# A two-layer streaming encoder on one core: the second layer's mixer is recorded and laid out as one planned order

## The chip, the core and the metric

The kernel runs on one core of one Trainium2 chip. The metric is device time of one execution in microseconds (us). All numbers are float32; matrix products run on TensorE (PE) in the fp32r form, and each product of float32 quality is made of three such products of split operands (high by high, high by low, low by high). VectorE is called DVE, ScalarE ACT, GpSimd POOL and SyncE SP, as in the profile. SP issues the weight loads; POOL issues small transfers.

## The reference, cut to what matters

One sequence of 512 tokens and 1024 features goes through two layers. Each layer adds a mixer, a cross-attention to 256 memory rows, and a gated ConvFFN to the stream `x`; only the mixers differ.

```
# layer 0: eight forgetting heads, four differential heads, one output projection
p = p1 - lam * p2
d_out = rms_norm(d_out, subln) * (1.0 - lambda_init)
mixed = concat(fox_out, d_out) @ w_out
# layer 1: mLSTM, four heads, chunkwise
qk = silu(causal_depthwise_conv(qk_pre, conv_qk))
h = mlstm_chunkwise(q, k, v, i_pre, log_f)
h = merge_heads(rms_norm(h, head_norm)) * sigmoid(og)
mixed = h @ w_out
```

So in both mixers a head's output is scaled by a root of its own mean square: four times in layer 0 (the differential heads), four times in layer 1.

## The kernel before, in words

**Stages.** `run` executes, per layer, a mixer (`mix0` or `mix1`) and then `rest` (cross-attention and ConvFFN). In the profiled execution `mix0` lies at about 0 to 253 us, `rest` of layer 0 at 253 to 714, `mix1` at 714 to 932 and `rest` of layer 1 at 932 to 1405.

**Tiles.** Activations stand as eight tiles of 128 features by 512 tokens, each as a high and a low part (`xh`, `xl`). A weight block of 128 by 1024 is loaded by SP into `raw`, cast by ACT to its high part `wh`, and DVE subtracts for the low part `wl` (`weight`, line 371; three buffers of each). A projection (`p_proj`, line 402) is 24 matmuls of 128x512 into one of four PSUM banks `acc` and is then evacuated by ACT and DVE. `p_proj_tok` (line 430) makes the values, 96 matmuls into all four banks.

**What sets the order.** Two things do. In `rest`, every instruction is a task of a list scheduler (`Sched`, line 180) with costs and due times, and the tasks are issued with `planned(True, 4)`: each instruction of DVE, ACT, POOL and SP then carries an ordering edge to the one before it on its engine, so the program's order is the order written down. In the two mixers a coarser planner (`Plan`, line 86) orders items of PE work with rough costs of the other engines, and issues a whole item at once; where the instructions of an item end up on their engine is then decided by the framework's own scheduler, which may move an instruction ahead of others that it does not depend on.

**The far norm.** `p_far_norm` (line 486) gets a head's 512 scale factors to all partitions by way of DRAM: PE sums squares, DVE makes `z`, POOL the root `y`; POOL issues a small DMA `roots<-y` to DRAM and a second DMA `hrb<-roots` (256 KB) that reads it back to all 128 partitions; then DVE multiplies by `hrb` (in layer 0 the row `ta<-ta,warm,hrb`), ACT casts the high part `mh`, and DVE subtracts for the low part `ml`. There is one buffer `hrb`, so the next copy waits until DVE has read the last. Line 507 calls `follow`: the next instruction on DVE gets an ordering edge to the instruction that was issued last there (or to a named one), so the framework's scheduler cannot move the multiplication ahead of it.

**Softmax of layer 0.** For each head and block of 128 queries PE writes scores to one of two PSUM banks `s`, DVE (the custom row with `sm`, shown as `ISA` in the order of instructions) adds the mask or bias and takes the extreme, ACT exponentiates, DVE takes the reciprocal, PE transposes, ACT or DVE copies to `pt`, and PE weighs the values. `p_qk` makes a head's keys: DVE `tmp<-acc,rb`, four ACT casts `ka`, two DVE subtractions `kb`.

**Mixer of layer 1.** Gate projection (`p_gate`, 16 matmuls), 96 matmuls for the first half of the values, then per head two projections with a convolution on DVE and ACT, two output gates, scores in the transposed form, a denominator and two numerators, a far norm (a near one for the last head), and at the end the output projection. Two blocks of the cross-attention's keys (`p_fill`) stand before the output projection. `p_memory` loads and splits the memory rows for that.

Of the kernel before, what the change touches and what calls it, by code (L numbers as in the profile page):

```python
# [9 lines left out]
F32 = mybir.dt.float32  # L10
# [22 lines left out]
MEM_AT, MEM_STEP = (140.0, 100), (24.0, 16.0)  # L33
FILLS, FILL_AT, FILL_PRIO = 2, (210.0, 140.0), 99
# [41 lines left out]
class Item:  # L76
    def __init__(self, fn, dur, deps, prio, take, free, chain, pre, after, order, load, st):
# [8 lines left out]
class Plan:  # L86
# [11 lines left out]
    def add(self, fn, dur=0.0, deps=(), prio=None, take=(), free=(), chain=(), pre=(), after=0.0, order=(), load=(), st=None, soon=False):  # L98
        it = Item(fn, dur, [d for d in deps if d is not None], len(self.items) if prio is None else prio, take, free, chain, pre, after, order, load, st)
        it.n, it.soon = len(self.items), soon  # L100
        self.items.append(it)
        return it

    def run(self):
        todo = sorted(self.items, key=lambda i: (i.prio, i.n))
        eng, t = self.eng, self.t
        while todo:
# [27 lines left out]
            for e, d in pick.pre:  # L135
                eng[e] = max(eng[e], t - 4.0) + d
            t += pick.dur
# [29 lines left out]
class Task:  # L167
    def __init__(self, eng, dur, fn, deps, prio, take, free, lat, after):
# [3 lines left out]
        self.take, self.free = take, free  # L172
# [3 lines left out]
WAIT = {"DVE": 0.4, "ACT": 0.3}  # L176
ONE, TWO, FORM, THEN = 4, 12, 10.0, (2, 1, 1)
OUT = (0, 4, 1, 5, 2, 6, 3, 7)

class Sched:  # L180
# [3 lines left out]
    def __init__(self, wait={}, **res):  # L184
        self.tasks, self.wait, self.held, self.ahead = [], wait, [], AHEAD
# [16 lines left out]
    def dues(self):  # L202
# [6 lines left out]
        for r, s in self.slots.items():  # L209
            takes = [(t, st) for t in self.tasks for q, st in t.take if q == r]  # L210
            if r == "acc":
                takes = [(None, st) for st in self.held] + takes
# [23 lines left out]
    def run(self):  # L236
# [7 lines left out]
        for t in self.tasks:  # L244
            for r, _ in t.take:
# [4 lines left out]
        while any(todo.values()):  # L250
            best = None
            for e, ts in todo.items():
                able = []
                for t in ts[:120]:
# [9 lines left out]
                    for j, (r, _) in enumerate(t.take):  # L264
                        if want[r][0] is not t:
# [18 lines left out]
            for r, st in t.take:  # L284
                want[r].pop(0)
# [10 lines left out]

class InOrder:
# [3 lines left out]
    def __init__(self, tc, engine):  # L301
        self.tc, self.engine = tc, engine
# [3 lines left out]
    def __getattr__(self, name):  # L306
        issue = getattr(self.engine, name)

        def call(*a, **k):
            i = issue(*a, **k)  # L310
# [7 lines left out]
    def follow(self, after=None):  # L318
        self.next = after or True


class Engines:
    def __init__(self, tc, names):
        self.nc = tc.nc
        self.chains = [InOrder(tc, getattr(tc.nc, n)) for n in names]
# [10 lines left out]

class Builder:
    def __init__(self, tc, t):
        self.tc, self.nc, self.t = tc, Engines(tc, ORDERED), t
# [12 lines left out]
    def til(self, pool, tag, shape=(P, 512), dtype=F32, bufs=None):  # L352
        return pool.tile(list(shape), dtype, tag=tag, name=self.nm(tag), bufs=bufs or 2)

# [47 lines left out]
    def p_proj(self, pl, src, xs, evac, chain, deps=(), kdeps=None, edeps=(), prio=None, n=SEQ, nk=KB8, order=None, etake=(), per=2, eorder=(), load=()):  # L402
# [5 lines left out]
        for c, e in zip(cuts, cuts[1:] + [nk]):  # L408
# [12 lines left out]
            for k in ks:  # L421
# [4 lines left out]
                pre=(("A", 0.12 * nk), ("D", 0.14 * nk)) if first else (), st=st,  # L426
            )
        return pl.add(lambda: evac(st["ps"]), 0, [last, *edeps], prio, take=etake, free=("acc",), chain=chain, order=eorder, load=load, st=st, soon=True)
# [92 lines left out]
    def p_out(self, pl, src, mixed, kdeps, gain, gi, order, prio, reload=False, order0=None):  # L521
# [3 lines left out]
        for m in range(KB8):  # L525
            e = self.p_proj(
                pl, src[m], mixed, lambda ps, m=m: self.xadd(m, ps, reload), (("D", 0.6),), kdeps=kdeps, order=order, prio=prio + m
# [192 lines left out]
    def split_rows(self, pool, *rows):  # L720

        t = pool.tile([P, SEQ], F32R, name=self.nm("rows"))
# [50 lines left out]
    def p_qk(self, pl, dq, dk, par, kdeps, edeps, prio):  # L773

        st = {}
        q = self.p_proj(
            pl, dq, self.xs, lambda ps: st.update(q=self.q_parts(ps)), (("D", 0.66), ("A", 0.52), ("D", 0.6), ("D", 0.6)), load=(("A", 0.52),),
# [3 lines left out]
            pl, dk, self.xs, lambda ps: st.update(k=self.k_parts(ps, par)), (("D", 0.6), ("A", 0.52), ("D", 0.6), ("D", 0.6)), load=(("A", 1.56),),  # L781
# [64 lines left out]

    def p_values(self, pl, src, edeps, prio, kdeps=None, ready=None):
# [28 lines left out]
    def mix0(self):  # L876
        nc, t, tc = self.nc, self.t, self.tc
        with tc.tile_pool(name="mix0", bufs=1, reuse_waits="tile") as mp:
            self.mp = mp
            self.kbt = [[mp.tile([P, 512], F32R, name=f"kb{s}{i}") for i in range(2)] for s in range(2)]  # L880
# [4 lines left out]
            sub8 = self.warm[:, 2:3]  # L885
            dmask = mp.tile([P, 512], F32, name="dmask")
            nc.vector.memset(dmask[:], 0.0)
            nc.vector.memset(dmask[0:64, 448:512], BIG)
            mh, ml = ([None if k in (2, 3) else mp.tile([P, SEQ], F32R, name=f"{n}{k}") for k in range(8)] for n in ("mh", "ml"))
# [4 lines left out]
            self.x = [self.xp.tile([P, SEQ], F32, name=f"x{k}", tag=f"x{k}") for k in range(KB8)]  # L894
# [74 lines left out]
            for h in range(4):  # L969
                p = 10 + 10 * h  # L970
                if h == 0:
                    v, ve = self.p_values(pl, t["dv"], [norm], p - 1, xk, [lambda: vw[1:], second])
                st, qk = self.p_qk(pl, t["dq"][h], t["dk"][h], h % 2, xk, [norm], p)
                pt = {}
                got = pl.add(lambda pt=pt: pt.update(t=self.til(mp, "pt", (P, 1536), bufs=3)), 0, qk, p + SOFT_PRIO, take=("pt",))
                ss, ts = [], []
                for i in range(4):
                    n = P * (i + 1)
                    bias = lambda n=n: dmask[:, 512 - n : 512]
                    r1, a1, b1 = self.p_soft(pl, st, 0, i, bias, qk, p + SOFT_PRIO)  # L980
# [1518 lines left out]
```

## Time and profile before

| | us |
|---|---|
| median of three runs | 1406.52 |
| lowest and highest of them | 1406.43, 1407.12 |
| the profiled execution's own time | 1407.05 |
| span of that execution | 1404.9 |

The span runs from the first instruction to the last; the 2.15 us between it and the execution's own time lie around it. The timeline's rows give start, duration, engine, line, operation, tiles and, in brackets, the idle time of the engine before the row and what ended it. A matmul's shown duration has a modelled end, so two matmuls in flight overlap in the rows; the distance between starts is what tells whether PE was kept waiting. In rows of DMA issues on POOL the shown duration is that of the issue, and the time to landing stands in the DMA view. Helper functions record every instruction under one line (L310), so groups are told apart by tiles.

### The profile page before, as it was taken

How to read it: one execution, taken by the hardware profiler on the slowest of the kernel's cores; microseconds unless marked ns; L12 is line 12 of the kernel's file. 1: busy time of each engine (PE TensorE's matmuls, PEld its weight loads, DVE VectorE, ACT ScalarE, POOL GpSimd, SP SyncE). 2: the span in 40 equal slices, each digit the busy share in tenths (PEclk: the TensorE clock that was granted, in tenths of full speed). 3: DMA queues.
4: the chain of work that ended last, by engine and by line, in shares of the span. 5: the costliest groups of instructions: out<-in, count | busy, mean ns of one | idle time of the engine just before them, and what ended most of it. 6: DMA issues, size and time to landing. Idle time of an engine off the chain costs nothing.

```text
span 1404.9 us, 23512 instructions
## 1 busy us (share of the span) xinstructions
PE 1390.2 (99%) x8876; PEld 1265.2 (90%) x8876; DVE 1186.4 (84%) x2042; ACT 874.4 (62%) x1486; POOL 146.8 (10%) x213
## 2 busy tenths in 40 slices
PE   9999999999999999999999999999999999999998
PEld 8888878899899999999888888989989999999997
DVE  7787786888799999999768876678878999999984
ACT  6797565666576665666456664456656866565555
POOL 0002230010011111011001120001000111110000
PEclk9999999999999999999999999999999999999999
DMA  6225324765567787674333332367464878776522
GB/s 207 91 53 154 117 68 151 246 188 158 158 145 191 211 199 187 151 200 106 86 108 105 129 98 83 120 188 240 136 185 114 196 201 204 182 185 168 154 66 81
DMA packets 80544, 211.06 MB, mean 150 GB/s; under 512 B 8640, under 2 KB 8640, under 8 KB 80432
## 3 DMA queue, kind: packets, MB, share of 16 engines
q1 hardware_dynamic: 63520, 165.02, 36.3%
q0 software_dynamic: 15904, 43.44, 17.7%
q8 instruction: 69, 1.13, 0.3%
q10 hardware_dynamic: 1008, 1.12, 0.2%
q14 instruction: 43, 0.35, 0.1%
HBM read 203.20 MB, written 6.34 MB: 149 GB/s over the span
## 4 chain that ended last, share of the span: by engine, by line
PE 85%; DVE 8%; ACT 3%; issue 2%; DMA 1%; POOL 1%; SPq 0%; POOLq 0%; DVEq 0%; ACTq 0%
PE acc L388 16%; PE acc L390 16%; PE acc L389 16%; PE w L388 4%; PE w L389 4%; PE w L390 4%; PE s L388 3%; PE s L390 3%; PE s L389 3%; PE acc L451 2%; PE acc L452 2%; PE acc L450 2%; DVE wl L310 1%; DVE qc L310 1%; PE w L2275 1%
## 5 line engine op out<-in xcount | busy, mean ns | idle before, releaser
L310 ACT CAST wh<-raw 128x1024 fp32r<-128x1024 f32 (+2 forms) x217 | 222.0, 1026 | 160.9 <-PE acc L389 76.4
L310 DVE TENSOR_TENSOR wl<-raw,wh 128x1024 fp32r<-128x1024 f32 (+2 forms) x217 | 259.6, 1198 | 39.2 <-ACT wh L310 37.9
L388 PE MATMUL acc<-xh,wh 128*128 128x256 f32 (+1 forms) x704 | 228.7, 325 | 0.0
L390 PE MATMUL acc<-xh,wl 128*128 128x256 f32 (+1 forms) x704 | 227.4, 323 | 0.5 <-DVE wl L310 0.5
L389 PE MATMUL acc<-xl,wh 128*128 128x256 f32 (+1 forms) x704 | 227.1, 323 | 0.0
L390 PEld LDWEIGHTS acc<-xh,wl 128*128 128x128 f32 x704 | 134.4, 191 | 9.3 <-DVE wl L310 0.9
L388 PEld LDWEIGHTS acc<-xh,wh 128*128 128x128 f32 x704 | 134.5, 191 | 7.6
L389 PEld LDWEIGHTS acc<-xl,wh 128*128 128x128 f32 x704 | 134.5, 191 | 7.5
L310 DVE SCALAR_TENSOR_TENSOR qc<-va,vec,qc 128x512 f32<-128x512 f32 x176 | 131.8, 749 | 6.9 <-ACT qc L310 4.0
L389 PE MATMUL acc<-f,k 128*128 128x256 f32 x336 | 92.5, 275 | 0.0
L390 PE MATMUL acc<-f,k 128*128 128x256 f32 x336 | 92.5, 275 | 0.0
L388 PE MATMUL acc<-f,k 128*128 128x256 f32 x336 | 92.5, 275 | 0.0
L310 ACT ACTIVATE qc<-va,vec 128x512 f32<-128x512 f32 x88 | 71.1, 812 | 19.2 <-DVE q L310 9.5
L388 PE MATMUL w<-q,wh 128*128 128x512 f32 x208 | 79.1, 380 | 0.6 <-ACT qc L310 0.6
L390 PE MATMUL w<-q,wl 128*128 128x512 f32 x208 | 78.9, 379 | 0.0
L389 PE MATMUL w<-q,wh 128*128 128x512 f32 x208 | 78.9, 379 | 0.0
L310 ACT ACTIVATE u<-acc 128x256 f32<-128x256 f32 x96 | 36.4, 379 | 68.1 <-PE acc L390 66.4
L390 PE MATMUL acc<-mem,wl 128*128 128x256 f32 (+1 forms) x236 | 73.8, 313 | 1.1 <-DVE wl L310 1.1
L388 PE MATMUL acc<-mem,wh 128*128 128x256 f32 (+1 forms) x236 | 73.9, 313 | 0.1
L389 PE MATMUL acc<-mem,wh 128*128 128x256 f32 (+1 forms) x236 | 73.7, 312 | 0.0
L310 DVE TENSOR_TENSOR x<-acc,x 128x512 f32<-128x512 f32 (+1 forms) x43 | 28.0, 653 | 47.2 <-PE acc L390 47.2
L310 ACT CAST k<-xe 128x512 fp32r<-128x512 f32 x84 | 51.0, 614 | 25.4 <-DVE xe L310 10.7
(414 smaller groups left out, 4207.0 us busy)
## 6 DMA issues: line engine op xcount, KB each, us to landing
raw<-in_up_dram SPq DMA_DIRECT2D x46, 512.0 KB, 4.3
raw<-in_down_dram SPq DMA_DIRECT2D x32, 512.0 KB, 4.6
sa<-in_up_dram SPq DMA_DIRECT2D x28, 512.0 KB, 5.1
sa<-in_up_dram POOLq DMA_DIRECT2D x28, 512.0 KB, 6.5
vb<-in_up_dram SPq DMA_DIRECT2D x42, 256.0 KB, 4.0
xe<-in_up_dram POOLq DMA_DIRECT2D x42, 256.0 KB, 4.8
raw<-in_wo_dram SPq DMA_DIRECT2D x16, 512.0 KB, 3.6
raw<-in_xk_dram SPq DMA_DIRECT2D x16, 512.0 KB, 3.9
```

The source lines that it names most:

```text
L310: i = issue(*a, **k)
L388: mm(out, wh, xh, start=first, stop=False, skip_group_check=parts)
L389: mm(out, wh, xl, start=False, stop=False, skip_group_check=parts)
L390: mm(out, wl, xh, start=False, stop=last, skip_group_check=parts)
L450: mm(ps, xh[k][:, ts], wh, start=(k == 0), stop=False)
L451: mm(ps, xh[k][:, ts], wl, start=False, stop=False)
L452: mm(ps, xl[k][:, ts], wh, start=False, stop=(k == 7))
L2275: nc.tensor.matmul(ps[:, lo:], vv[s][:, c], a[:], start=(s == 0), stop=(s == 3))
```

## The change

The text adds a layer between the mixers' code and the engines. `Ref` and `View` stand for tiles that are not yet allocated. A `Recorder` stands in for the four engines and PE: in recording mode it makes a task of every instruction, with costs per engine and kind, dependencies from the tiles' regions, and a ring of buffers per tag; at the end the list scheduler that `rest` uses orders all tasks of all five engines and issues them with `planned(True, 4)`. In direct mode the recorder issues the instruction at once, as before. `BEGIN` sets from which planner time on a mixer is recorded: 1e9 for layer 0, which is never reached, and 0 for layer 1. So `mix0` has a recorder attached but stays in direct mode, and `mix1` is recorded whole.

Beside it: `follow` does nothing while a recorder is attached, in direct mode too; the order numbers of layer 1's items come from tables (`PROJ1`, `SOFT1`, `NORM1`, `GATE1`, `V1`, `EARLIES1`) in place of sums; layer 1's memory rows are loaded at planner time 20 instead of 100, and its two blocks of keys may start at 44 instead of 140; in layer 0 the buffer `kb` is taken from a list instead of by the head's parity. The tables of layer 0 hold the values that the sums gave. No arithmetic changes: each engine has the same instructions in the same numbers, in another order.

```diff
-MEM_AT, MEM_STEP = (140.0, 100), (24.0, 16.0)
-FILLS, FILL_AT, FILL_PRIO = 2, (210.0, 140.0), 99
+MEM_AT, MEM_STEP = (140.0, 20), (24.0, 4.0)
+FILLS, FILL_AT, FILL_PRIO = 2, (210.0, 44.0), 99
...
+SOFT1, NORM1 = [-28, 6.5, 39.5, 58], [11, -7.5, 21.5, 2.5]
...
+BEGIN, EARLY = (1e9, 0.0), 0.0
...
+    def item(self, t, it):
...
+        if self.direct and t >= self.at:
+            self.direct = False
+            self.clock = self.start = t
+            self.b.nc.planned(True, 4)
...
+    def add(self, eng, issue, name, a, k):
+        (outs, ins), out = self.views(name, a, k)
+        dur, lat = self.cost(eng, name, out, a, k)
...
+        if self.direct:
+            fn()
+            t = Task(E, dur, None, (), 0.0, (), (), lat, 0.0)
+            t.end, t.n = self.at, -1
...
+            t = self.sc.add(E, dur, None, (), self.clock - self.early + (0.0 if E == "PE" else 3.0), lat=lat)
...
+    def run(self):
+        sc = self.sc
...
+        self.b.rec = self.b.nc.record(None)
+        sc.run()
+        self.b.nc.planned(False, 4)
...
         def call(*a, **k):
-            i = issue(*a, **k)
+            if self.rec and not self.rec.issuing:
+                return self.rec.add(self.name, call, name, a, k)
+            i = issue(*map(real, a), **{w: real(v) for w, v in k.items()})
...
     def follow(self, after=None):
-        self.next = after or True
+        if not self.rec:
+            self.next = after or True
...
         with tc.tile_pool(name="mix0", bufs=1, reuse_waits="tile") as mp:
             self.mp = mp
+            self.rec = Recorder(self, 0)
+            self.pars = [0, 1]
...
         with tc.tile_pool(name="mix1", bufs=1, reuse_waits="tile") as mp:
             self.mp = mp
+            self.rec = rec = Recorder(self, 1)
...
+            pl.rec = self.rec
             pl.run()
-            self.plan = pl
+            rec = self.rec
+            rec.run()
```

**What moved on DVE in layer 0, at the second and third far norm.** The names: `hrb` is the copied scale, `ta` a head's output, `mem` and `sq` the split of the memory rows and their squares, `tmp` and `kb` a head's keys, `ISA` the softmax row on scores `s`. Before, this stretch of DVE has no far norm in it:

```order
L310 TENSOR_TENSOR sq_1594<-sq_1594,sqt_1756 128x256
L310 SCALAR_TENSOR_TENSOR mem_1755<-raw_1591,vec,mem_1755 128x256
L310 TENSOR_TENSOR tmp_1371<-acc_264_1342,rb_335 128x512
L310 TENSOR_TENSOR wl_1558<-raw_1556,wh_1557 128x1024
L310 TENSOR_TENSOR kb_114<-tmp_1371,ka_268_1373 64x512
L310 TENSOR_TENSOR kb_116<-tmp_1371,ka_269_1377 64x512
L310 ISA x_137,sm_1417<-s_1410,tb_1411 128x128
```

The same stretch of DVE now:

```order
L606 TENSOR_TENSOR sq_1591<-sq_1591,sqt_1754 128x256
L606 SCALAR_TENSOR_TENSOR ta_1254<-ta_1254,warm,hrb_1349 128x512
L606 SCALAR_TENSOR_TENSOR mem_1757<-raw_1589,vec,mem_1757 128x256
L606 TENSOR_TENSOR tmp_1371<-acc_264_1342,rb_335 128x512
L606 TENSOR_TENSOR wl_1558<-raw_1554,wh_1556 128x1024
L606 TENSOR_TENSOR kb_114<-tmp_1371,ka_268_1373 64x512
L606 TENSOR_TENSOR ml_134<-ta_1254,mh_128 128x512
L606 TENSOR_TENSOR kb_116<-tmp_1371,ka_269_1377 64x512
L606 SCALAR_TENSOR_TENSOR ta_1263<-ta_1263,warm,hrb_1400 128x512
L606 ISA x_137,sm_1415<-s_1412,tb_1408 128x128
```

The multiplications of the second and third differential head stand some thirty rows earlier than before, ahead of the keys and the first scores of the next pair of heads; their subtraction `ml` came with them. On ACT the casts `mh` moved likewise, one ahead of the four casts `ka`, one ahead of the table load for the exponentials.

**On POOL, at the same place**, the copies `hrb` and the masked biases `tb` before:

```order
L310 DMA roots_1363<-y_1324 128x4
L310 DMA hrb_1349<-roots_1327 128x512
L310 AFFINE_SELECT tb_1436<-fb_1310 128x256
L310 AFFINE_SELECT tb_1445<-fb_1312 128x256
L310 AFFINE_SELECT tb_1484<-fb_1310 128x384
```

and now:

```order
L606 DMA roots_1363<-y_1325 128x4
L606 DMA hrb_1349<-roots_1327 128x512
L606 DMA hrb_1400<-roots_1363 128x512
L606 AFFINE_SELECT tb_1433<-fb_1310 128x256
L606 AFFINE_SELECT tb_1442<-fb_1312 128x256
```

The third head's copy follows the second's at once; it stood eight rows later. The first head's multiplication moved in the same way by some forty rows, to the row after a `tmp`, and the fourth's by some twenty, to the row behind two copies to `pt`.

**On SP, at the start of the second mixer**, where `mv`, `mqk` and `mog` are weights of values, queries and keys, and output gates, before:

```order
L310 DMA raw_8324<-in_mv_dram 128x1024
L310 DMA raw_8362<-in_mqk_dram 128x1024
L310 DMA raw_8415<-in_mqk_dram 128x1024
L310 DMA raw_8461<-in_mqk_dram 128x1024
L310 DMA raw_8519<-in_mqk_dram 128x1024
```

and now:

```order
L606 DMA raw_8159<-in_mv_dram 128x1024
L606 DMA raw_8182<-in_mem_dram 128x1024
L606 DMA raw_8186<-in_mem_dram 128x1024
L606 DMA raw_8239<-in_mqk_dram 128x1024
L606 DMA raw_8252<-in_mqk_dram 128x1024
```

The two loads of memory rows stand ahead of the first query and key weights; the first of them stood behind ten further loads. On PE the 16 gate matmuls and the norm of `x` moved from ahead of the first values to behind them; the 24 matmuls of each projection stay together, with scores between them at other places than before.

More of the change, by code (lines that the diff above doesn't have):

```diff
@@ L76, with __init__ @@
 class Item:
-    def __init__(self, fn, dur, deps, prio, take, free, chain, pre, after, order, load, st):
+    def __init__(self, fn, dur, deps, prio, take, free, chain, pre, after, order, load, st, due=None, behind=(), late=False):
+        self.due, self.behind, self.late, self.tasks = due, behind, late, []
         self.fn, self.dur, self.deps, self.prio, self.st = fn, dur, list(deps), prio, st
@@ L244, in run @@
         for t in self.tasks:
[L245 removed]
+            for r, _ in t.take if not t.loose else ():
                 want[r].append(t)
```

445 lines of the change are left out of this document (372 added, 73 removed).

## The prediction

> **What bounds the kernel now.** I read the page first, then busy time by stage, then who keeps PE waiting, and last the timelines around the instructions that the change moves.
>
> ```profile
> span 1404.9 us, 23512 instructions
> ...
> PE 1390.2 (99%) x8876; PEld 1265.2 (90%) x8876; DVE 1186.4 (84%) x2042; ACT 874.4 (62%) x1486; POOL 146.8 (10%) x213
> ```
>
> PE is busy all the time, so the kernel is PE's matmuls, and time comes or goes only where PE is kept waiting. By stage, with the length of the stretch ahead of PE's busy time:
>
> ```profile
> 253.00:714.00 461.00, 459.83 (x3213) 432.48 (x3212) 418.39 (x659) 289.46 (x482) 45.32 (x55) 1.00 0.64 170
> 714.00:932.00 218.00, 216.44 (x1063) 185.36 (x1061) 158.18 (x238) 120.02 (x172) 22.79 (x42) 1.00 0.35 108
> ```
>
> The second row is the mixer that the change records: PE stands for 218.00 - 216.44 = 1.56 us in it. A wait shows only beyond the modelled end of the last matmul, about 0.16 later than the rhythm of the starts; with some ten short waits the true loss is at most about 1.56 + 1.6 = 3.2. That bounds what a better order of this mixer can win: 3.2 us of 1406.5, hardly above the 0.2% (2.8 us) that a measurement of this kernel can tell from no change. The waits that PE has there:
>
> ```profile
> PE s L388 <- ACT k L310: 0.8, 1, 0.8
> ...
> PE s L547 <- DVE hsq L310: 0.6, 1, 0.6
> ```
>
> PE waits for the first keys and for one sum of squares. The other half of the argument lies in layer 0, which is not meant to change: there `follow` no longer works, and the four far norms stand earlier on DVE. What matters is when their tiles land. The copies are issued on POOL here:
>
> ```profile
> 88.60 0.59 POOL L310 DMA_DIRECT2D hrb<-roots  x1 [1.94 <-DMA roots<-y]
> ...
> 129.75 0.54 POOL L310 DMA_DIRECT2D hrb<-roots  x1
> ...
> 142.62 0.54 POOL L310 DMA_DIRECT2D hrb<-roots  x1 [0.63 <-DVE ta L310]
> ...
> 159.94 0.57 POOL L310 DMA_DIRECT2D hrb<-roots  x1 [1.96 <-DMA roots<-y]
> ```
>
> and take, in the same order, the time at the end of each row from issue to landing:
>
> ```profile
> hrb<-roots POOLq DMA_DIRECT2D x1, 256.0 KB, 4.5
> hrb<-roots POOLq DMA_DIRECT2D x1, 256.0 KB, 5.9
> hrb<-roots POOLq DMA_DIRECT2D x1, 256.0 KB, 5.1
> hrb<-roots POOLq DMA_DIRECT2D x1, 256.0 KB, 3.9
> ```
>
> So they land at 93.1, 135.65, 147.7 and 163.84. The POOL instructions ahead of the first, second and fourth keep their order, so these three issues keep their times; only the third moves.
>
> **Second and third far norm.** DVE before, with the new places behind the first of these rows and ahead of the row at 133.70:
>
> ```profile
> 128.72 0.42 DVE L310 TENSOR_TENSOR sq<-sq,sqt 128x256 f32<-128x256 f32 x1
> 129.06 0.48 DVE L310 SCALAR_TENSOR_TENSOR mem<-raw,vec,mem 128x256 fp32r<-128x256 f32 x1
> 129.48 0.69 DVE L310 TENSOR_TENSOR tmp<-acc,rb 128x512 f32<-128x512 f32 x1
> ...
> 131.49 1.40 DVE L310 TENSOR_TENSOR kb<-tmp,ka 64x512 fp32r<-64x512 f32 x2
> 133.70 0.29 DVE L310 CUSTOM_DVE_ANT_0 x<-s,tb 128x128 f32<-128x128 f32 x1 [0.82 <-PE s L798]
> ...
> 135.01 0.42 DVE L310 CUSTOM_DVE_ANT_0 x<-s,tb 128x256 f32<-128x256 f32 x1
> ...
> 141.60 0.73 DVE L310 SCALAR_TENSOR_TENSOR ta<-ta,warm,hrb 128x512 f32<-128x512 f32 x1
> ```
>
> ACT and PE in the same stretch:
>
> ```profile
> 130.22 2.55 ACT L310 CAST ka<-tmp 64x512 fp32r<-64x512 f32 x4
> 132.79 1.28 ACT L310 ACT_TABLE_LOAD   x1
> 134.08 0.40 ACT L310 ACTIVATE x<-x,sm 128x128 f32<-128x128 f32 x1
> ...
> 142.36 0.62 ACT L310 CAST mh<-ta 128x512 fp32r<-128x512 f32 x1
> ```
> ```profile
> 133.17 0.27 PE L798 MATMUL s<-ka,qa 128*128 128x256 f32 x1
> ...
> 134.26 0.27 PE L798 MATMUL s<-ka,qa 128*128 128x256 f32 x1
> ...
> 136.65 0.33 PE L798 MATMUL s<-ka,qa 128*128 128x384 f32 x1
> ```
>
> The second multiplication now follows the row at 128.72. DVE gets there at 129.06 and stands until the tile lands at 135.65: 6.6 us. Behind it are queued the last memory row, `tmp`, a weight's low part, the keys `kb` and all softmax rows; PE waits for the keys, and ACT for `tmp`. Step by step from 135.65: multiplication 0.73, to 136.4; memory row 0.42 (129.06 to 129.48), to 136.8; `tmp` 0.69, to 137.5; four casts 2.55, to 140.0; the second `kb` to about 140.4. DVE then stands at the third multiplication. Its copy needs the buffer, so POOL issues it 0.3 after the second multiplication ends (before: 141.60 + 0.73 = 142.33, then 142.62), at 136.7, and it lands 5.1 later, at 141.8; the multiplication ends at 142.5. On ACT the cast `mh` (0.62, to 143.1) and the table load (1.28, to 144.4) come ahead of the first exponential; from that to the softmax row of the third score block were 135.01 - 134.08 = 0.93, I take 0.7, as one small row between now stands elsewhere, so it runs at 145.1 and frees its bank at 145.5. The fifth score block of PE, at 136.65 before, needs that bank: 145.5 - 136.65 = 8.9 us lost. PE's own order is unchanged here and has no work that it may take instead. POOL's copy also holds back the masked biases behind it, until 137.3; they wait for DVE's softmax rows anyway, so that costs nothing. Bounds: with 3.9 for both landings the same chain gives 5.7, with 5.9 for both 9.7.
>
> **First far norm.** The row now follows the first of these:
>
> ```profile
> 90.11 0.68 DVE L310 SCALAR_TENSOR_TENSOR tmp<-acc,rb 128x512 f32<-128x512 f32 x1
> 90.71 0.41 DVE L310 CUSTOM_DVE_ANT_0 x<-s,dmask 128x256 f32<-128x256 f32 x1
> ```
> ```profile
> 90.19 0.38 PE L450 MATMUL acc<-wh,xh 128*128 128x512 f32 x1
> 90.41 0.38 PE L451 MATMUL acc<-wl,xh 128*128 128x512 f32 x1
> 91.18 0.43 PE L798 MATMUL s<-ka,qa 128*128 128x384 f32 x1 [0.40 <-DVE sm L310]
> ```
>
> DVE stands from 90.8 to the landing at 93.1, then runs the multiplication (0.73), a copy of probabilities and the softmax row (0.41), which frees the bank at 94.45 with 0.2 allowed for the copy, which is half as wide as the softmax row's 0.41. PE's score at 91.18 needs it: 3.27 later. In the new order three more projection matmuls stand ahead of that score, and 94.45 less their 3 x 0.216 (the distance of PE's starts, 90.19 to 90.41) leaves 2.6 us. Bounds by landings of 3.9 and 5.9: 2.0 and 4.0.
>
> **Fourth far norm.** It stood at the last of these rows of DVE and now stands between the first two; PE's rows in the same stretch follow:
>
> ```profile
> 160.41 1.02 DVE L310 COPY pt<-w 128x384 f32<-128x384 f32 x2
> 161.64 0.29 DVE L310 CUSTOM_DVE_ANT_0 x<-s,tb 128x128 f32<-128x128 f32 x1 [0.20 <-PE s L799]
> ...
> 168.23 0.69 DVE L310 TENSOR_TENSOR tmp<-acc,rb 128x512 f32<-128x512 f32 x1 [2.96 <-PE acc L390]
> ...
> 173.23 0.73 DVE L310 SCALAR_TENSOR_TENSOR ta<-ta,warm,hrb 128x512 f32<-128x512 f32 x1
> ```
> ```profile
> 161.55 0.38 PE L388 MATMUL acc<-xh,wh 128*128 128x512 f32 x1
> ...
> 168.03 0.60 PE L831 MATMUL w<-ident,x 128*128 128x128 f32 x4
> ```
>
> DVE stands from 161.4 to 163.84, and the softmax row comes at 164.6 instead of 161.64, 2.95 late. PE has projection matmuls from 161.55 until the transposes at 168.03, and DVE was idle for 2.96 ahead of 168.23: the cover is just as long as the delay. I take 0; were the cover half as long, 0.9 and more would show, so 0.9 is the upper bound. The four multiplications and subtractions are gone from where they stood, among softmax rows for which PE waits now and then: I take -0.6 for that, less than one multiplication (0.73), and twice that as a bound.
>
> **The second mixer.** PE's work is the same; the order is planned with costs of all engines. The stretch from 253 to 714 is laid out by the same scheduler and keeps PE standing for 461.00 - 459.83 = 1.17 in more than twice the length, so I take it that the 1.56 goes: -1.5. Where an instruction moved past queues: the two memory loads on SP now stand ahead of the query weights, which PE needs only behind 96 matmuls of values (20.7 us at 0.216) and 16 of the gates; eight small rows on ACT and DVE come with them in the same cover. The gate weights' DMA leaves layer 0's start on ACT for this cover too. The gates move behind the values; by the order, 165 matmuls (35.6 us) remain between them and the first scores. All three cost nothing while the values hide them; if they hid nothing, each would cost a landing like the 3.9 to 5.9 above, which I don't believe. A planned order with wrong costs can make waits like the 0.8 for `k` above at each of the four heads: upper bound +4; lower bound -3.2.
>
> **The sum.** 8.9 + 2.6 + 0 - 0.6 - 1.5 = +9.4. The profiled execution: span 1404.9 + 9.4 = 1414.3, with the 2.15 around the span 1416.4; the median of the runs is 0.53 below the profiled execution, so 1415.9 us.
>
> **Rivals.** *The copies land sooner*, as DVE stands still while they run. At 3.5, the least of the seven copies of the kernel,
>
> ```profile
> DMA to landing us min/median/max: 3.5/4.5/5.9
> ```
>
> the first place costs 1.6, the second 5.2, and the sum is +4.7: 1411.2. The Trainium skill, "DMA: Bandwidth & Descriptors", section "Anatomy of one DMA", gives a DMA issued by GpSimd about 2.0 us plus its bytes over 436 GB/s; for 256 KB that is an estimate of 2.6 us, by which the places would cost 0.7 and 4.3 and the time would be 1409.4. The four rows above, 3.9 to 5.9, speak against so short a landing.
>
> *The planned order of the second mixer adds waits*, +4 instead of -1.5: 1421.4. For it speaks that its tables were never timed in this trace; against it the 1.17 of the stage laid out the same way.
>
> *Faster*: the waits in layer 0 stay hidden behind PE's projections and the second mixer loses all its waits: 1406.5 - 3.2 - 0.6 = 1402.7. The point that decides is the second copy: PE's score at 133.17 follows `tmp` (129.48) by 3.7 and the keys took about 3.4, so the tile would have to land by about 129.4. Its DMA is issued at 129.75. Only a DVE that gets there far later could hide it.
>
> *Nothing that can be measured*: the moved rows find their tiles landed since DVE is late for other reasons, and the second mixer is as before: within 1406.5 +- 2.8.
>
> **How the numbers follow.** Forecast 0.62, the sooner landing 0.08, more waits in the second mixer 0.15, faster 0.06, nothing measurable 0.09. Slower by over 0.2%: 0.62 + 0.15 + 0.08 = 0.85; within 0.2%: 0.09; faster: 0.06. All terms at their lower ends give 5.7 + 2.0 - 1.2 - 3.2 = +3.3, that is 1409.8; at their upper ends 9.7 + 4.0 + 0.9 + 4 = +18.6. The range reaches down to 1409.0, just under the low ends and the estimate by the page, and up to the rival with more waits, 1421.5; it leaves out the two cases without a loss and the far upper end.
>
> **What would show it.** Right, if in the new profile DVE's waits for `hrb` from DMA come to some 10 us in layer 0 (6.6, 1.4, 2.3 and 2.4 by place), PE's busy time between 84 and 178 us falls behind by about 11, and in the second mixer PE stands for less than 1.5. Wrong, if the multiplications start without waiting, if PE passes the scores at 133 and 136 within a microsecond of before, or if the second mixer gains or loses over 4.

## The result

| | before | after |
|---|---|---|
| median, us | 1406.47 (4 runs, 1405.86 to 1407.12) | 1419.77 (4 runs, 1418.31 to 1420.17) |
| ratio to before, 95% interval | | 1.0093 (1.008 to 1.0105) |
| span of the profiled execution, us | 1404.9 | 1417.9 |
| mean granted clock of PE in it | 1.00 | 0.994 |

The kernel became slower by 13.3 us; 1415.9 was forecast, in a range of 1409.0 to 1421.5. Where the time went is read from equal matmuls. The first matmul of the cross-attention ends a mixer, once per layer. First the two rows of the kernel before, then those of the changed one:

```profile
253.06 0.38 PE L1386 MATMUL acc<-wh,mem 128*128 128x512 f32 x1
...
931.03 0.38 PE L1386 MATMUL acc<-wh,mem 128*128 128x512 f32 x1
```
```profile
262.70 0.38 PE L606 MATMUL acc<-wh,mem 128*128 128x512 f32 x1
...
943.63 0.38 PE L606 MATMUL acc<-wh,mem 128*128 128x512 f32 x1
```

Layer 0's mixer is 9.64 us later at its end. From there to the end of the second mixer it was 677.97 us and is now 680.93, so the second mixer (the stage between is unchanged) cost 2.96 more. The rest of the 13.0 us of span (0.4) lies in the last stage.

**Layer 0.** The four copies on POOL and the four multiplications on DVE in the changed kernel:

```profile
87.73 0.58 POOL L606 DMA_DIRECT2D hrb<-roots  x1 [1.77 <-DMA roots<-y]
...
132.58 0.54 POOL L606 DMA_DIRECT2D hrb<-roots  x1
...
137.07 0.54 POOL L606 DMA_DIRECT2D hrb<-roots  x1 [3.96 <-DVE ta L606]
...
169.30 0.57 POOL L606 DMA_DIRECT2D hrb<-roots  x1 [2.07 <-DMA roots<-y]
```
```profile
92.04 0.75 DVE L606 SCALAR_TENSOR_TENSOR ta<-ta,warm,hrb 128x512 f32<-128x512 f32 x1 [1.95 <-DMA hrb<-roots]
...
136.03 0.75 DVE L606 SCALAR_TENSOR_TENSOR ta<-ta,warm,hrb 128x512 f32<-128x512 f32 x1 [4.03 <-DMA hrb<-roots]
...
141.96 0.75 DVE L606 SCALAR_TENSOR_TENSOR ta<-ta,warm,hrb 128x512 f32<-128x512 f32 x1 [1.14 <-DMA hrb<-roots]
...
173.60 0.75 DVE L606 SCALAR_TENSOR_TENSOR ta<-ta,warm,hrb 128x512 f32<-128x512 f32 x1 [2.54 <-DMA hrb<-roots]
```

DVE stands at each of the four for the landing, 9.7 us together. A copy lands 3.4 to 4.9 us after its issue (92.04 - 87.73 = 4.3, then 3.4, 4.9, 4.3). The third copy is issued when the second multiplication has freed the buffer. PE waits behind the first and the second:

```profile
93.38 0.43 PE L606 MATMUL s<-ka,qa 128*128 128x384 f32 x1 [2.65 <-DVE sm L606]
...
135.62 0.38 PE L606 MATMUL acc<-xh,wl 128*128 128x512 f32 x1
139.12 0.58 PE L606 MATMUL s<-ka,qa 128*128 128x256 f32 x1 [3.12 <-ACT ka L606]
...
141.25 0.63 PE L606 MATMUL acc<-xh,wh 128*128 128x512 f32 x1
141.68 0.63 PE L606 MATMUL acc<-xl,wh 128*128 128x512 f32 x1
...
146.69 0.33 PE L606 MATMUL s<-ka,qa 128*128 128x384 f32 x1
```

The matmul at 141.25 shows what the prediction did not foresee: the next one starts 0.43 behind it, where matmuls of this size started 0.216 apart before. The length of the stretch, PE's busy time and, third from the end, the granted clock of three stretches say why:

```profile
90.00:96.00 6.00, 3.35 (x13) 2.49 (x12) 3.80 (x17) 4.36 (x13) 0.00 (x0) 0.86 0.25 70
...
138.00:144.00 6.00, 4.38 (x12) 2.93 (x12) 4.57 (x10) 3.51 (x6) 0.76 (x2) 0.56 0.71 220
144.00:150.00 6.00, 6.00 (x27) 5.25 (x27) 5.06 (x18) 5.63 (x15) 1.96 (x4) 0.87 0.10 18
```

Behind both long waits PE runs at half its clock: the same view gives 0.50 for 94.30 to 97.71 and for 138.68 to 145.50. By an estimate from these lengths that costs 1.7 us behind the first and up to 3.4 behind the second, on top of the waits, as far as nothing else holds PE up meanwhile.

**The second mixer.** Who keeps PE waiting there now:

```profile
PE s L606 <- DVE hsq L606: 1.2, 1, 1.2
PE acc L606 <- DVE wl L606: 0.7, 1, 0.7
PE s L606 <- DVE at L606: 0.7, 2, 0.4
```

The names: `hsq` is a sum of squares, `at` the weighted scores, `cv` a convolution's output (and, later, a part of the sum for the denominator), `sg` an output gate, `kl` the low part of a head's keys. The wait for `hsq` grew from 0.6 to 1.2, the 0.8 for `k` went, three others came (those for `wl` and `at`, and 0.2 for `cv`), and the longest is again followed by a stretch at half clock, 0.50 from 835.00 to 838.41; the starts of equal matmuls are 0.43 apart instead of 0.216 from 835.07 to 838.06:

```profile
831.88 0.38 PE L606 MATMUL acc<-xh,wl 128*128 128x512 f32 x1
833.49 1.05 PE L606 MATMUL s<-ones,hsq 128*128 128x2 f32 x8 [1.23 <-DVE hsq L606]
...
835.07 0.63 PE L606 MATMUL acc<-wl,xh 128*128 128x512 f32 x1
835.50 0.63 PE L606 MATMUL acc<-wh,xl 128*128 128x512 f32 x1
...
838.06 0.56 PE L606 MATMUL acc<-wh,xl 128*128 128x512 f32 x1
838.45 0.38 PE L606 MATMUL acc<-wh,xh 128*128 128x512 f32 x1
```

### The profile page after: what moved, and what is told of

Read it like the earlier page. It is cut to its first block, busy times and chain, and to the rows that moved or that the text cites. A ratio compares the mean times of both kernels' runs of the same rounds, so it can differ in the third digit from the quotient of the medians.

```text
span 1417.9 us, 23514 instructions
## 1 busy us (share of the span) xinstructions
PE 1396.5 (98%) x8876; PEld 1269.0 (89%) x8876; DVE 1185.6 (84%) x2042; ACT 873.9 (62%) x1486; POOL 150.2 (11%) x213
## 4 chain that ended last, share of the span: by engine, by line
PE 81%; DVE 10%; ACT 3%; issue 2%; DMA 2%; POOL 1%; POOLq 0%; DVEq 0%; ACTq 0%
PE acc L606 54%; PE w L606 16%; PE s L606 11%; DVE wl L606 2%; DVE cv L606 1%; DVE qc L606 1%; DMA hrb<-roots 1%; DVE va L606 1%; DVE x L606 1%; DVE sm L606 1%; DMA raw<-in_xv_dram 1%; DVE f L606 0%; ACT wh L606 0%; DMA fb<-decays 0%; DVE mk L606 0%
## 5 line engine op out<-in xcount | busy, mean ns | idle before, releaser
L606 PE MATMUL acc<-f,k 128*128 128x256 f32 x1008 | 126.1, 275 | 0.0
L606 PE MATMUL w<-q,wh 128*128 128x512 f32 x416 | 123.9, 379 | 0.6 <-ACT qc L606 0.6
L606 PEld LDWEIGHTS acc<-f,k 128*128 128x128 f32 x1008 | 121.4, 192 | 1.5
L606 PE MATMUL acc<-mem,wh 128*128 128x256 f32 (+1 forms) x472 | 102.4, 313 | 0.1
L606 PEld LDWEIGHTS w<-q,wh 128*128 128x128 f32 x416 | 75.3, 190 | 9.7 <-ACT qc L606 1.0
L606 PEld LDWEIGHTS acc<-mem,wh 128*128 128x128 f32 x472 | 78.0, 191 | 5.0 <-ACT wh L606 0.5
L606 PE MATMUL acc<-f,wh 128*128 128x256 f32 x384 | 66.8, 275 | 0.0
L606 PE MATMUL s<-f,wh 128*128 128x256 f32 x384 | 66.7, 275 | 0.0
L606 POOL DMA_DIRECT2D xe<-in_up_dram x42 | 36.7, 875 | 278.2 <-DVE k L606 201.6
```

The source lines that it names most:

```text
L606: i = issue(*map(real, a), **{w: real(v) for w, v in k.items()})
```

## The experiments

Theory A: the lost ordering edges cost layer 0 some 9.6 us, and the planned second mixer costs 3 on its own. The rivals stand in each expectation. Each time is a median of 4 to 11 runs, beside the kernel before on the same chip (1406.2 to 1406.6).

| kernel | us | over before | ratio to before, 95% |
|---|---|---|---|
| the changed kernel | 1419.77 | 13.3 | 1.0093 (1.008 to 1.0105) |
| e1_edges_back | 1409.68 | 3.3 | 1.0024 (1.0014 to 1.0034) |
| e2_edges_off_alone | 1416.28 | 9.9 | 1.0075 (1.0062 to 1.0087) |
| e3_first_edge_back | 1416.05 | 9.7 | 1.0068 (1.0055 to 1.0081) |
| e4_two_buffers | 1418.89 | 12.5 | 1.0093 (1.0079 to 1.0107) |
| e5_tables_unplanned | 1408.20 | 2.0 | 1.0014 (1.0005 to 1.0023) |
| e6_landing_counted | 1408.41 | 2.2 | 1.0016 (1.0007 to 1.0025) |
| e7_fed | 1408.96 | 2.8 | 1.0019 (1.001 to 1.0028) |
| e8_layer0_planned | 1408.81 | 2.6 | 1.0019 (1.001 to 1.0027) |
| e9_fed_layer0 | 1420.74 | 14.1 | 1.0098 (1.0083 to 1.0114) |
| e10_memory_later | 1411.39 | 4.8 | 1.0033 (1.002 to 1.0045) |
| e11_middle_edges_back | 1413.27 | 6.8 | 1.0045 (1.0033 to 1.0058) |
| e12_masks_dearer | 1412.86 | 6.4 | 1.004 (1.0027 to 1.0054) |

### The two halves of the change, apart: e1 and e2

e1 is the changed kernel with `follow` at work in direct mode:

```diff
     def follow(self, after=None):
-        if not self.rec:
+        if not self.rec or self.rec.direct:
             self.next = after or True
```

> Layer 0 in the order of before (its four far norms follow their edges again), second mixer planned as in the changed kernel. In the two traces the offset between equal matmuls is 9.65 us behind layer 0 and 13.1 behind the second mixer. Theory A (the lost edges cost 9.65, the planned second mixer 3.5): 1406.5 + 3.5 = 1410.0, no wait for hrb above 2 us in layer 0. Rival B (the second mixer's loss is only a late echo of layer 0, such as transfers or a clock that came late): 1406.5. Rival C (the planned mixer is what costs, layer 0 only a little): 1415 or more.

e2 is the kernel before without the edges of layer 0:

```diff
         def last():
-            nc.vector.follow(state.get("behind"))
+            if not self.mixing0:
+                nc.vector.follow(state.get("behind"))
             fin(st["rb"])
```

> The kernel before with the four edges of layer 0 left out and nothing else; second mixer as before. Theory A: 1406.5 + 9.65 = 1416.1, with DVE waits for hrb of about 2, 4, 1 and 2.5 us and two stretches at half clock behind the two long PE waits. Rival B (the stretches at half clock are chance and do not belong to the waits): about 4 us less, 1412. Rival C: 1407 to 1410.

Measured: 1409.68 and 1416.28, where theory A had 1410.0 and 1416.1. The order of instructions makes this a clean pair: e1's layer 0 is the one before (but for a DMA of gate weights that moved away) and its second mixer the changed one, e2's the other way round. By the same two matmuls, e2's layer 0 ends at 262.08 and its way to the end of the second mixer is 677.97 us, as before to the hundredth; e1's layer 0 ends at 252.31, and the way is 681.11. The two losses are independent and add up: 3.3 + 9.9 = 13.2 of 13.3. In e2 the granted clock is 0.50 from 94.24 to 97.65 and from 138.61 to 145.44, behind the same two waits as in the changed kernel. Rivals B and C fall.

### The places of layer 0: e3, e11, e4

e3 brings back the edge of the first head alone, e11 those of the second and third alone; `BACK` is `(1,)` or `(2, 3)`, on top of e1's edit:

```diff
-            nc.vector.follow(state.get("behind"))
+            if self.rec and self.rec.direct:
+                self.fars = getattr(self, "fars", 0) + 1
+            if not (self.rec and self.rec.direct) or self.fars in BACK:
+                nc.vector.follow(state.get("behind"))
```

> The changed kernel with the edge of the first head alone back, so the second, third and fourth multiplications stay early. Theory A: the first place costs 3.4 us in the trace (excess of PE's start to start from 84 to 120 us, 4.75 against 1.38), so 1419.8 - 3.4 = 1416.4. Rival (the wait is only handed on, the second place's wait grows by what the first gives back): 1419 to 1420.

> The changed kernel with the edges of the second and third head back, the first and the fourth multiplication early. If the places add up: all edges back measured 1409.7 and the first edge back alone 1416.05, so the places behind the first cost 6.4; the first costs 1419.8 - 1416.05 = 3.7, and this kernel comes to 1409.7 + 3.7 = 1413.4 if the fourth place costs nothing, up to 1414.3 if it costs 0.9. Rival (one wait pays for the other): below 1411.5.

Measured: 1416.05 and 1413.27. Over before, the first place costs 13.3 - 9.7 = 3.6, the places behind it 9.7 - 3.3 = 6.4, and e11 shows that they add: 3.3 + 3.6 = 6.9 against its 6.8. So the waits are not handed on, and the fourth place costs nothing: in e11 DVE's fourth multiplication waits for its copy at 167 us, and PE's busy time from 120 to 178 us (second fence) is whole:

```profile
167.27 0.75 DVE L607 SCALAR_TENSOR_TENSOR ta<-ta,warm,hrb 128x512 f32<-128x512 f32 x1 [3.31 <-DMA hrb<-roots]
```
```profile
120.00:178.00 58.00, 58.00 (x311) 49.51 (x310) 43.77 (x111) 40.33 (x78) 17.55 (x29) 1.00 0.47 137
```

e4 gives the copies of layer 0 a second buffer in the changed kernel:

```diff
-(mp, "hrb", (P, SEQ), F32, 1), scaled, [w], soft,
+(mp, "hrb", (P, SEQ), F32, 2), scaled, [w], soft,
```

> The changed kernel with two buffers for hrb in layer 0 in place of one, the same order on every engine. The third copy is then issued right behind the second instead of 4 us later. Theory A: the third multiplication's wait of 1.1 us goes, and PE gets up to 1.1 back: 1418.7 to 1419.1. Rival (two copies at once share the transfer and the second lands that much later): 1419.8 or more.

Measured: 1418.89, 0.8 to 0.9 less, as theory A had it, but well inside the intervals. The trace is clearer: on POOL the third copy follows the second by 1.7 us and no longer waits for DVE, and DVE's third multiplication starts without a wait:

```profile
131.23 0.54 POOL L606 DMA_DIRECT2D hrb<-roots  x1
132.91 0.54 POOL L606 DMA_DIRECT2D hrb<-roots  x1 [1.14 <-DMA roots<-y]
```
```profile
134.59 0.75 DVE L606 SCALAR_TENSOR_TENSOR ta<-ta,warm,hrb 128x512 f32<-128x512 f32 x1 [4.10 <-DMA hrb<-roots]
...
139.42 0.75 DVE L606 SCALAR_TENSOR_TENSOR ta<-ta,warm,hrb 128x512 f32<-128x512 f32 x1
```

Both landed after 3.3 to 3.4 us, so two copies in flight did not slow each other. What the one buffer costs is about 1 us; the second copy's own landing is what costs.

### The second mixer: e5, e6, e10, e12

The cause of the wait for `hsq` is read in e1, where the mixer is undisturbed by layer 0: POOL, then ACT, then DVE.

```profile
813.74 0.60 POOL L606 DMA_DIRECT2D roots<-y  x1 [0.31 <-POOL y L606]
817.30 0.56 POOL L606 DMA_DIRECT2D hrb<-roots  x1 [2.96 <-DMA roots<-y]
817.86 0.87 POOL L606 TENSOR_SCALAR_AFFINE_SELECT mk<-mxb 128x384 f32<-128x384 f32 x2
```
```profile
818.41 0.61 ACT L606 ACTIVATE mk<-mk,ucol 128x384 f32<-128x384 f32 x1 [2.10 <-POOL mk L606]
...
821.03 1.12 ACT L606 ACTIVATE th<-num 128x512 f32<-128x512 f32 x1
```
```profile
822.54 0.68 DVE L606 TENSOR_TENSOR hsq<-hsq,th 128x512 f32<-128x512 f32 x1
```

In the planned order the copy `hrb` follows the small DMA `roots` at once. POOL stands 2.96 us for its landing, two masks stand behind it, ACT waits 2.10 for a mask (`mk`) in front of the squares (`th`), and the sum that PE needs ends at 823.2. The planner does not see this: for two tasks on the same engine it takes the latency between them as zero, and here that latency is a transfer's landing. e6 counts it, for POOL in the recorded mixer, on top of e1:

```diff
-                        at = max(at, d.end + (0.0 if d.eng == e else d.lat))
+                        at = max(at, d.end + (0.0 if d.eng == e and not (self.landed and e == "POOL" and d.lat > 1.0) else d.lat))
```

> Edges of layer 0 back, second mixer planned, and the planner counts the landing of a DMA also when the next instruction is on the same queue (POOL). Two masks then stand ahead of the first copy hrb, one ahead of the second; nothing outside the second mixer changes. Theory P: the 1.4 us wait of PE for hsq near 822 us shrinks below 0.7 and the half-clock stretch behind it goes: 1406.5 to 1408.2. Rival (the two multiplications by hrb and the squares on ACT set that wait): 1409.7 as with the edges back alone.

(`landed` is set for the recorder's scheduler alone.) Measured: 1408.41, 2.2 over before where e1 has 3.3. The intervals overlap, so the time alone doesn't settle it; the trace does. The way to the end of the mixer is 679.58 us (252.19 to 931.77), 1.5 less than e1's; the masks use the time of the landing, the wait for `hsq` is gone, and no stretch at half clock follows. From POOL in e6:

```profile
813.59 0.60 POOL L608 DMA_DIRECT2D roots<-y  x1 [0.31 <-POOL y L608]
814.21 1.83 POOL L608 TENSOR_SCALAR_AFFINE_SELECT mk<-mxb 128x384 f32<-128x384 f32 x2
817.03 0.58 POOL L608 DMA_DIRECT2D hrb<-roots  x1 [0.99 <-DMA roots<-y]
```

So the trace shows this mechanism. Its price is 1.1 in the medians and 1.5 in the two traces, of 3.3; with overlapping intervals that is less sure than the mechanism. What is left sits in other waits of e6 (0.7 for `wl` and 0.7 for `at` as in e1, and a new one of 1.0 for `sg`). e5 asks whether the planning or the new numbers bring it; it is e1 with

```diff
-BEGIN, EARLY = (1e9, 0.0), 0.0
+BEGIN, EARLY = (1e9, 1e9), 0.0
```

> Edges of layer 0 back, and the second mixer issued directly (not recorded), but with its new order numbers, early memory rows and early key blocks. The kernel with the edges back and the planned mixer measured 1409.7, before 1406.4. Theory P (the planned order of all engines costs the 3.3 us: POOL's copy hrb, planned as if the small DMA in front of it landed at once, holds back the masks): 1406 to 1408. Theory T (the new order numbers and due times cost it, whoever orders the engines): 1409 to 1411.

Measured: 1408.20, between the two theories. Without a plan the new numbers still cost 2.0, by another wait (once 1.6 us, for `cv` of ACT). Neither theory holds alone: some 2 of the 3.3 stay where nothing is planned.

e10 and e12 change one thing each in e6. e10 loads the memory rows later, e12 raises POOL's costs in the planner:

```diff
-MEM_AT, MEM_STEP = (140.0, 20), (24.0, 4.0)
+MEM_AT, MEM_STEP = (140.0, 80), (24.0, 4.0)
```

> As with the landing counted (1408.4), but the memory rows of the second mixer are loaded at planner time 80 in place of 20, so that SP's two loads stand behind eight query and key weights again, as before the change, and ACT's and DVE's splits come later. The prediction took the early loads as free: then 1407.5 to 1409.3, and PE's 0.7 us wait for wl near 762 us stays. Rival (the early loads hold up the first query weights): that wait goes and the time falls by 0.7 or more, to 1407.7 or less.

```diff
-        return {"affine_select": 0.55, "tensor_tensor": 1.1}.get(name, 0.1), 0.25
+        return {"affine_select": 1.0, "tensor_tensor": 1.4}.get(name, 0.1), 0.25
```

> As with the landing counted (1408.4), and the planner takes 1.0 us for a mask on POOL in place of 0.55 and 1.4 for its power in place of 1.1, nearer to the 0.4 to 1.0 and 1.2 to 1.4 of the traces. If too low costs of POOL bring PE's 0.7 us of waits for at near 782 us: 1407.5, at best level with the kernel before at 1406.5. Rival (any other order of this mixer brings its own waits): 1408 to 1411.

Measured: 1411.39 and 1412.86. Of e10 neither side had expected a loss, and e12 is beyond what its rival had. In e10 PE waits 1.7 us once for `at`, in e12 2.3 once for `wh`:

```profile
PE s L608 <- DVE at L608: 1.7, 1, 1.7
```
```profile
PE acc L608 <- ACT wh L608: 2.3, 1, 2.3
PE acc L608 <- DVE sg L608: 1.0, 1, 1.0
```

So taking the early memory loads back is no cure: it costs 2.6 more. As the planner lays out the whole mixer anew, that isn't the price of the loads alone. Dearer POOL costs made no better order either. They were not nearer to the trace throughout: in e6 the sixteen masks take 0.74 us on average, between 0.55 and 1.0, and the five powers 1.44. All five orders (e1, e5, e6, e10, e12) have one to three waits of 1 us and more, the longest of each at another place; which of the new numbers brings the 2 us that e5 and e6 keep is not settled.

### The clock: e7 and e9

e7 is e1 with extra matmuls in the wait for `hsq`. Their results are overwritten, so nothing of the output changes:

```diff
         ps = self.bank("b")
+        if self.rec and self.rec.layer:
+            self.sums = getattr(self, "sums", 0) + 1
+            for _ in range(FEED if self.sums == FEED_AT else 0):
+                self.nc.tensor.matmul(ps[:], self.xh[0][:, :P], self.xh[0][:], start=True, stop=True)
```

> Edges of layer 0 back, second mixer planned, and six extra matmuls of 128x512 (1.3 us, their results are overwritten) ahead of the second head's sums of squares, where PE stands for 1.4 us near 822 us. Theory K (PE's standing brings the half clock, 1.7 us of loss): PE no longer stands, no half-clock stretch follows, 1408.0, and the runs lie closer together than the 1407.7 to 1412.2 without the matmuls. Rival (the half clock comes by chance or by load): 1409.7 to 1410, the same stretch at half clock.

Measured: 1408.96, 2.8 over before against e1's 3.3, where theory K had 1.7 less; the two intervals overlap. For the mechanism the trace decides: PE waits 0.20, and the matmuls behind it stay at 0.38.

```profile
821.77 1.55 PE L607 MATMUL s<-xh 128*128 128x512 f32 x6
823.53 1.05 PE L607 MATMUL s<-ones,hsq 128*128 128x2 f32 x8 [0.20 <-DVE hsq L607]
...
825.17 0.38 PE L607 MATMUL acc<-wh,xh 128*128 128x512 f32 x1
```

All eleven runs of e7 have a granted clock of 0.999 or 1.0; of the nine of e1 three have 0.999 and take 1407.7 to 1408.8, five 0.998 and 1409.6 to 1410.7, one 0.997 and 1412.2. One stretch of 3.4 us at half clock takes 0.0012 off the mean clock of a run, an estimate from these lengths. So the clocks suggest that e1's stretch does not come in each run; only one of them was profiled. Feeding PE brings the runs closer together, over 2.7 us in place of 4.5, and saves 0.5 to 0.7 on the median, less than the 1.7 of the profiled run. In the traces e7's way to the end of the mixer is 679.64 us (252.34 to 931.98), 1.5 less than e1's and level with e6's 679.58. As e7 still spends the wait, on useless matmuls, what it saves should be the half clock alone. So most of e6's 1.5 may be the half clock too, with the wait itself made up for by e6's new wait for `sg`; no run here separates the two.

e9 does the same in the changed kernel at the second far norm, with 14 matmuls ahead of the score at 139 us (`FEED, FEED_AT = 14, 33`):

```diff
             ps = self.bank("s")
+            self.scores = getattr(self, "scores", 0) + 1
+            for _ in range(FEED if self.scores == FEED_AT else 0):
+                nc.tensor.matmul(ps[:], self.xh[0][:, :P], self.xh[0][:], start=True, stop=True)
             b = bias()
```

> The changed kernel with 14 extra matmuls of 128x512 (3.0 us, their results are overwritten) in layer 0, ahead of the score at 139 us for which PE stands 3.3 us in the changed kernel. DVE reaches the keys no sooner. Theory K (PE's standing brings the half clock): the wait becomes useless work, the clock stays whole behind it, and the some 5 us of matmuls that ran at half clock up to 145.5 take 2.5 less: 1419.8 - 2.5 = 1417.3, granted clock 1.00 from 138 to 150 us. Rival (the clock drops for another reason, or extra matmuls only cost): 1419.8 or more.

Measured: 1420.74, so no gain; the rival's number, but extra matmuls aren't all that the edit brought. The clock of the two stretches, which were 0.56 and 0.87:

```profile
138.00:144.00 6.00, 3.33 (x13) 1.91 (x11) 4.38 (x7) 3.77 (x6) 0.00 (x0) 1.00 0.67 218
144.00:150.00 6.00, 5.85 (x22) 5.03 (x23) 5.14 (x21) 4.85 (x13) 2.01 (x5) 0.72 0.00 1
```

Kept busy, PE has its whole clock at 138 to 144. The half clock comes behind the next wait instead, for the softmax rows that follow DVE's third multiplication:

```profile
141.56 0.38 PE L607 MATMUL acc<-xh,wl 128*128 128x512 f32 x1
144.15 0.38 PE L607 MATMUL s<-ka,qa 128*128 128x256 f32 x1 [2.21 <-DVE sm L607]
```

In the changed kernel this score starts at 142.98, after a wait of 0.24. PE got there sooner in e9, but DVE's softmax row came later too. First the changed kernel, then e9:

```profile
142.63 0.28 DVE L606 CUSTOM_DVE_ANT_0 x<-s,tb 128x128 f32<-128x128 f32 x1
```
```profile
141.76 0.75 DVE L607 SCALAR_TENSOR_TENSOR ta<-ta,warm,hrb 128x512 f32<-128x512 f32 x1 [0.90 <-DMA hrb<-roots]
143.20 0.69 DVE L607 TENSOR_TENSOR ml<-ta,mh 128x512 fp32r<-128x512 f32 x1 [0.69 <-ACT mh L607]
143.81 0.28 DVE L607 CUSTOM_DVE_ANT_0 x<-s,tb 128x128 f32<-128x128 f32 x1
```

In the changed kernel the subtraction `ml`, which needs ACT's `mh`, stands behind the first two softmax rows. In e9 the framework's scheduler put it ahead of them, so the first runs 1.2 us later though the multiplication is 0.2 earlier. So e9 changed DVE's order as well as PE's work. It shows that PE's standing brings the half clock; what the half clock costs at this place it doesn't show.

### Layer 0 planned too: e8

e8 is e6 with

```diff
-BEGIN, EARLY = (1e9, 0.0), 0.0
+BEGIN, EARLY = (120.0, 0.0), 0.0
```

> As with the landing counted, and layer 0's mixer recorded and planned too from planner time 120, that is from about the second half of it. Between 178 and 253 us PE loses 6.15 us to waits in the kernel before. If a planned order helps where there are waits: 2 to 4 us less than with the landing counted alone, 1403 to 1406. Rival (the tables of layer 0 are the old sums, and the plan adds waits as it did in the second mixer): 1409 or more.

Measured: 1408.81, level with e6. PE is busy for 70.94 of the 75 us from 178 to 253, where it was 72.06 in e6 and before: the plan won nothing there, and the rival's added waits are small. No kernel here beats the one before.

## Why the prediction was right, point by point

**The mechanism of layer 0** was right. e2 shows that the lost edges alone cost 9.9 us, and the chain ran as laid out: DVE stands for the second copy, the keys and ACT's casts come late, and the third copy, issued 0.3 behind the second multiplication (136.03 + 0.75, then 137.07), holds the softmax rows. The price by place, from equal matmuls: 24.09 before and 23.38 now at the start (-0.7), 118.97 and 121.64 behind the first place (+2.67, so 3.4 for it), 136.65 and 146.69 behind the second and third (+10.04, so 7.4).

- *Second and third norm, +8.9 (5.7 to 9.7)*: 7.4 in the trace, 6.4 by e3 less e1. The issues did not keep their times, since the first place had held everything back (the second copy went out at 132.58, not 129.75). The two copies landed after 3.4 and 4.9, not 5.9 and 5.1; with these landings the prediction's chain gives 8.9 - 2.5 - 0.2 = 6.2. The half clock, which it did not have, can stand for the rest. The list of waits foreseen for DVE (6.6, 1.4, 2.3, 2.4, which make 12.7 and not "some 10") became 4.0, 1.1, 1.95 and 2.5, together 9.7.
- *First norm, +2.6 (2.0 to 4.0)*: 3.4 in the trace, 3.6 by e3. PE's wait grew from 0.40 to 2.65, which is 2.25; the rest lies in the stretch at half clock behind it.
- *Fourth norm, 0*: 0, by e11.
- *Relief, -0.6*: not shown. The -0.7 of the trace is there at 24 us already, ahead of the first norm. It belongs to the one profiled execution of the kernel before and not to the change: there ACT waits 0.66 at 7.48 for a block of value weights. e2, whose start is that of the kernel before, has the same matmul at 23.35, and e10, whose start is that of the changed kernel, at 24.14.

**The second mixer, -1.5**, is the step that failed: in place of a gain, it cost 3.0 in the trace, and e1, which has it alone, is 3.3 slower. The argument took the waits of a stage laid out by the same planner as a measure. That stage has no far norm, and so not this pair of DMAs ahead of masks; by e6 the landing that the planner leaves out is 1.1 to 1.5 of it, with the half clock behind the wait, and what brings the rest is open. The rival "the planned order adds waits, +4", with a chance of 0.15, was nearer; the four waits of 0.8 that it named make 3.2.

**The clock** was in no term. The profile of before shows 1.00 in each stage, and no wait of PE in it is as long as the two of layer 0 here. In the changed kernel the half clock follows the wait. The Trainium skill, "TensorE: Matmul & The Clock Gate", section "HAM oscillation — how this bites in real kernels", tells of it: a PE that idles too long falls to half its clock, and the section puts the limit at gaps of about 3.4 us. The trace disagrees on the limit: the gap ahead of 833.49 was 1.23 us, and in e1 1.37. How long it lasts here, 835.07 to 838.45 or 3.4 us, agrees with the warm-up of about 3.4 us that section "Part 1: The HAM clock gate" of that page gives; the stretch behind 138.68 is twice as long.

The rival *the copies land sooner* was half right, since the second landed after 3.4. The prediction's estimate of 2.6 us from the Trainium skill, "DMA: Bandwidth & Descriptors", section "Anatomy of one DMA", is below every copy measured, 3.3 and more.

**The signs and the sum.** Of the signs that were named, DVE's waits came, 9.7 us for some 10. PE's busy time between 84 and 178 us fell behind by 5.6 and not 11 (93.37 before, 87.73 now); PE counts as busy at half clock, and the granted clock there is 0.95. In the second mixer PE stands for 219.80 - 216.97 = 2.83 us (723.70 to 943.50), not for less than 1.5. The sum came out 3.6 too low for the span: 1.3 too much for layer 0 (10.9 against 9.64, of which 0.7 is the late start in the profiled execution of the kernel before), 4.5 too little for the second mixer, and 0.4 in the last stage. So that 1415.9 came as near as it did is in part luck. Its errors have both signs; in layer 0 shorter landings and a half clock that was not foreseen offset each other; and it is the rival with more waits that carries the range up to 1421.5.

## What to carry to other kernels

When a recorder or another layer is put around code, look for what it switches off: here an ordering edge that nobody meant to touch cost three times what the meant change did (9.9 and 3.3), and it is easier to see in the order of instructions than in the text of the change. A planner that takes latencies between tasks of one queue as zero must make an exception for a transfer that waits for another transfer. And on a PE that is otherwise always busy a wait may cost a stretch at half clock beside its own length: in e1 1.4 us of wait, and about 1.5 more by e7.

## What the hardware showed

- Short waits can halve PE's clock. Counted as start to start beyond the normal rhythm, the traces of this case have 19 waits of PE of 1.3 us and more. Behind 16 of them the granted clock was 0.50, for 3.4 us or, four times, 6.8; among them are 1.39 (changed kernel), 1.54 (e1) and 1.68 (e9). Behind 2.72 in e4, 1.74 in e5 and 1.37 in e9 it stayed whole, and so it did behind the longest of the kernel before, 1.26. So the length alone doesn't decide it. Runs of a kernel with such waits can differ more: e1's spread over 4.5 us, those of the kernel before beside it over 1.7.
- A copy of 256 KB from POOL landed in 3.4 to 4.9 us in layer 0 of the changed kernel, and in e4 two of them 1.7 us apart in 3.3 and 3.4.
- The DMA `roots`, 2 KB, landed after 1.7 to 3.3 us in e1's second mixer, hardly less than such a copy at worst. Behind the one of 3.3 POOL went on 3.56 us after the issue (813.74 to 817.30).
